# Offset parts of the norms behind the rotary tables, one row's norm offset on VectorE, and a nine-instruction inverse root in a two-layer decoder trunk

## The chip, the cores and the metric

The kernel runs on one core of a Trainium2 chip. Its engines are named as in the profile: PE (TensorE: matmuls and transposes), DVE (VectorE), ACT (ScalarE), POOL (GpSimd) and SP (SyncE, which here only issues transfers). Each engine takes its instructions in the order in which they were written into its queue. The metric is the time of one execution on the device in microseconds (us), the median of several runs.

## The reference

A trunk of two layers over 1024 tokens of width 1024, in float32. Layer 0 is a sparse attention: an indexer scores all earlier keys, each query keeps the best 256, and softmax attention runs on those. Layer 1 is a gated linear recurrence (HGRN2). Both are followed by a SwiGLU feed-forward part, and every part ends in a LayerNorm of `alpha * x + part(x)`. What the change touches:

```python
def layer_norm(x, g, b):
    mu = jnp.mean(xf, axis=-1, keepdims=True)
    var = jnp.mean(jnp.square(xf - mu), axis=-1, keepdims=True)
    return (xf - mu) * lax.rsqrt(var + LN_EPS) * g + b
...
def apply_rope(x, cos, sin):          # on the first dimensions of queries, keys and index keys
    return jnp.concatenate([x1 * cos - x2 * sin, x2 * cos + x1 * sin, x[..., 2 * half:]], axis=-1)
...
cos_q, sin_q = rope_tables(positions, ATT_ROT_DIM)      # from the positions, an input
c_q = rms_norm(c_q, g_cq)                               # another inverse root
k_idx = layer_norm(k_idx, g_ik, b_ik)
```

## The kernel before

The tokens lie in 8 row blocks of 128 (the partitions). Every float32 product is made of three products of rounded parts (lines 110 to 112, `mm3`), and the dense parts use a scheme of seven block products per 2 by 2 blocks, for which rows and weights are first added and subtracted in 512-column pieces and each result is split into a rounded part and a rest (lines 471 and 472, `split2`).

The program is written as Python generators that call engine instructions. A scheduling layer places the instructions of the engines' queues from the order of writing, with priorities and dependences; it also inserts the waits. So a shift in one place can shift neighbours on other engines.

**The start (`att_in`).** `rope_tables` (line 170) makes the cosine and sine tables: DVE reduces the angles, ACT takes the sine (line 206; the cosine first, then the sine), and POOL copies each table into its second half (line 207) and, twice, every other column into a shorter table (line 209). The shorter tables rotate the keys. Then a written list, `ORDER_IN`, sets the steps: `p` projects a row block (tile A), `f` transposes the next input rows, `k` handles the keys of a pair of row blocks. The key step takes an inverse root (`rsqrt`, line 114, tiles aih, aiy, ait), rotates the keys (`rope`, lines 221 to 225, tile rk), splits them (tile kk: ACT at line 1328, DVE at 1329) and lets PE transpose them (line 1343), then the normalized query part and the index keys (tile hc, lines 1351 and 1354). Ahead of each step of `ORDER_IN` one step of the generator `kits` is advanced.

**The offset parts (`kits`, line 378).** For two of the norms the bias b is later added to products by small matmuls instead of row by row. For that, POOL prepares five small tables in memory: first `select`, rows of ones (line 388, three transfers at 390), then four kits, two of them times a factor (line 399): load 4 rows (396), a difference and a negation (400, 401), and three times round to bfloat16 (404), store (405) and subtract (408). All use one work tile, `za`, so a step waits for the transfer of an earlier one. The tables are read by the feed-forward and later parts.

**The end of attention (`layer_norm`, line 135).** Rows 0 to 5 are normalized while the last attention blocks run, rows 6 and 7 after them. For each: DVE subtracts the mean and multiplies by g (line 151), ACT multiplies by the inverse root (152), POOL adds b in two halves (154). Then `enter` begins the first feed-forward part: `row_sums` (374, 375, tile gb) takes the sums of the row pairs (4, 6) and (5, 7) on DVE, and PE transposes rows and sums (line 352), whose split parts (tiles x_1617 to x_1620, one for each group of operands) feed the products.

**The inverse root (`rsqrt`).** It works on a few numbers per partition: scale and add eps (line 118), a first estimate from the bits of the number (119), three Newton steps of three instructions (121 to 123). Each depends on the one before. It is used at the four key pairs, the three groups of `layer_norm`, the norms of the later parts (`norm_scale`) and eight times in the recurrence (tile rm).

Of the kernel before, what the change touches and what calls it, by code (L numbers as in the profile page):

```python
# [18 lines left out]
ALU = mybir.AluOpType  # L19
# [48 lines left out]
class Core:  # L68
# [45 lines left out]
    def rsqrt(self, x, n, scale, eps, tag, eng=None):  # L114

        v = eng or self.nc.vector
        h, y, t = (self.tile(self.small, [P, max(n, 4)], F32, tag + x)[:, :n] for x in "hyt")
        v.tensor_scalar(h, x, scale, eps, op0=ALU.mult, op1=ALU.add)
        v.tensor_scalar(y.bitcast(I32), h.bitcast(I32), -0.5, 1597463007.0, op0=ALU.mult, op1=ALU.add)
        for _ in range(3):  # L120
            v.tensor_tensor(t, y, y, op=ALU.mult)
            v.scalar_tensor_tensor(t, t, -0.5, h, op0=ALU.mult, op1=ALU.mult)
            self.root = v.scalar_tensor_tensor(y, t, 1.5, y, op0=ALU.add, op1=ALU.mult)
        return y

    def pin(self, ins):
# [8 lines left out]
    def layer_norm(self, ts, g, b):  # L135

        nc, v = self.nc, self.nc.vector
        n = len(ts)
        mv = self.tile(self.small, [P, 4, 2], F32, "lnmv")[:, :n]
        for i, t in enumerate(ts):  # L140
            r = self.resid[:, t, :]
            st = self.tile(self.small, [P, 2, 6], F32, "lnst")
            for c in range(2):
                v.bn_stats(st[:, c, :], r[:, c * 512 : (c + 1) * 512])
            v.bn_aggr(mv[:, i, :], st.rearrange("p a b -> p (a b)"))
            yield
        rs = self.rsqrt(mv[:, :, 1], n, 1.0, LN_EPS, "ln")
        yield
        for i, t in enumerate(ts):
            r = self.resid[:, t, :]  # L150
            v.scalar_tensor_tensor(r, r, mv[:, i, 0:1], g, op0=ALU.subtract, op1=ALU.mult)
            nc.scalar.activation(r, r, AF.Copy, scale=rs[:, i : i + 1])
            for c in (slice(0, 512), slice(512, D)):
                nc.gpsimd.tensor_tensor(r[:, c], r[:, c], b[:, c], op=ALU.add)
            yield

    def row(self):
# [10 lines left out]
    def rope_tables(self, cp, wp, pt, it):  # L168

        nc, v = self.nc, self.nc.vector  # L170
        n = NT * 16
        pf = self.tile(wp, [P, NT], F32, "posf")
        v.tensor_copy(pf, pt)
        three = self.tile(wp, [P, 3, n], F32, "kk")
        ang, a1, a2 = (three[:, i, :] for i in range(3))
        v.tensor_tensor(
            ang.rearrange("p (t j) -> p t j", t=NT),
            pf.rearrange("p (t o) -> p t o", o=1).to_broadcast([P, NT, 16]),
            it.rearrange("p (o j) -> p o j", o=1).to_broadcast([P, NT, 16]),
            op=ALU.mult,  # L180
        )
        v.tensor_copy(a1.bitcast(F32R), ang)
        v.tensor_tensor(a2, ang, a1, op=ALU.subtract)
        turns = self.tile(wp, [P, 7, n], F32, "q")
        near = self.tile(wp, [P, 7, n], F32, "qi")
        for i, (a, p) in enumerate(((a1, 3), (a2, 2), (a1, 2), (a2, 1), (a1, 1), (a2, 0), (a1, 0))):
            v.tensor_scalar(turns[:, i, :], a, TURN[p], None, op0=ALU.mult)

        def frac(x, tmp, magic):
            v.tensor_scalar(tmp, x, magic, magic, op0=ALU.add, op1=ALU.subtract)  # L190
            v.tensor_tensor(x, x, tmp, op=ALU.subtract)

        frac(turns, near, 1.5 * 2.0**35)
        frac(turns, near, 1.5 * 2.0**23)
        u = turns[:, 0, :]
        for i in range(1, 7):
            v.tensor_tensor(u, u, turns[:, i, :], op=ALU.add)
        tabs = []
        for i, off in enumerate((0.25, 0.0)):
            w = turns[:, 1 + i, :]  # L200
            v.tensor_scalar(w, u, off, None, op0=ALU.add)
            frac(w, near[:, 0, :], 1.5 * 2.0**23)
            v.tensor_scalar(w, w, -0.4999999, 0.4999999, op0=ALU.max, op1=ALU.min)
            o, e = (self.tile(cp, [P, NT, 2, n], F32, f"rope{i}{n}") for n in (16, 8))
            w = w.rearrange("p (t j) -> p t j", t=NT)
            nc.scalar.activation(o[:, :, 0, :], w, AF.Sin, scale=2.0 * math.pi)
            nc.gpsimd.tensor_copy(o[:, :, 1, :], o[:, :, 0, :])
            for j in range(2):
                nc.gpsimd.tensor_copy(e[:, :, j, :], o[:, :, 0, 0:16:2])
            tabs.append((o, e))  # L210
        return zip(*tabs)

# [165 lines left out]
    def kits(self, pool, work, bs):  # L378

        nc, gp = self.nc, self.nc.gpsimd
        self.select = self.tile(self.kd, [12, 512], BF16, "select")
        self.kit = {}
        y = work[0:4, 0:256].bitcast(BF16)
        ones = self.ident[0:4, 0:4].rearrange("p (k o) -> p k o", o=1).to_broadcast([4, 4, P])
        gp.tensor_copy(y.rearrange("p (k c) -> p k c", k=4), ones)
        for j in range(3):
            gp.dma_start(self.select[4 * j : 4 * j + 4], y)  # L390
        yield
        rest, part = work[0:4, 0:512], work[0:4, 512:1024].bitcast(BF16)
        four = rest.rearrange("k (i c) -> k i c", i=4)
        for b, name, scale in bs:
            o = self.kit[name] = self.tile(self.kd, [12, 512], BF16, self.name(name[0]))
            gp.dma_start(four[:, 0:2, :], b.rearrange("(i k c) -> k i c", i=2, k=4))
            yield
            if scale is not None:
                gp.tensor_scalar(four[:, 0:2, :], four[:, 0:2, :], scale, None, op0=ALU.mult)
            gp.tensor_tensor(four[:, 2, :], four[:, 0, :], four[:, 1, :], op=ALU.subtract)  # L400
            gp.tensor_scalar(four[:, 3, :], four[:, 1, :], -1.0, None, op0=ALU.mult)
            for j in range(3):
                x = part[:, j % 2 * 512 : (j % 2 + 1) * 512]
                gp.tensor_copy(x, rest)
                gp.dma_start(o[4 * j : 4 * j + 4], x)
                yield
                if j < 2:
                    gp.tensor_tensor(rest, rest, x, op=ALU.subtract)
# [809 lines left out]
    def att_in(self, ap, csp, tp, x):  # L1218
        nc, v, gp, s = self.nc, self.nc.vector, self.nc.gpsimd, self.att
# [199 lines left out]

        does = dict(p=project, f=feature, k=keys, q=query, s=store, w=lambda _: query_weights(), a=lambda _: advance())  # L1420
        kits = self.kits(ap, self.tile(s.sel, [P, T], F32, "za"), s.bs)
        for step in self.ORDER_IN.split():
            next(kits, None)
            does[step[0]](int(step[1:] or 0))

    @staticmethod
# [608 lines left out]
```

## Time and profile before

| what | value |
|---|---|
| time, median of 3 runs | 2513.41 us (2510.82 to 2516.71) |
| the profiled execution | 2517.95 us, its span 2516.2 us |
| PE busy in the span | 2441.9 us |
| DVE busy | 1906.9 us |
| ACT busy | 1056.2 us |
| POOL busy | 176.9 us |

Times in profile rows count from the start of the span. A row of the order of time has the start, the duration, the engine, the line of the kernel, the instruction, its output and inputs with partitions x elements, how many follow each other (x), and in brackets how long the engine stood idle before it and which instruction ended that. Line numbers in rows of before are those of the kernel before; after the change, lines from `pin` on are 4 higher, up to `ORDER_IN`'s loop, and 5 higher behind it.

### The profile page before, as it was taken

How to read it: one execution, taken by the hardware profiler on the slowest of the kernel's cores; microseconds unless marked ns; L12 is line 12 of the kernel's file. 1: busy time of each engine (PE TensorE's matmuls, PEld its weight loads, DVE VectorE, ACT ScalarE, POOL GpSimd, SP SyncE). 2: the span in 40 equal slices, each digit the busy share in tenths (PEclk: the TensorE clock that was granted, in tenths of full speed). 3: DMA queues.
4: the chain of work that ended last, by engine and by line, in shares of the span. 5: the costliest groups of instructions: out<-in, count | busy, mean ns of one | idle time of the engine just before them, and what ended most of it. 6: DMA issues, size and time to landing. Idle time of an engine off the chain costs nothing.

```text
span 2516.2 us, 35546 instructions
## 1 busy us (share of the span) xinstructions
PE 2441.9 (97%) x12810; PEld 2041.3 (81%) x12810; DVE 1906.9 (76%) x3692; ACT 1056.2 (42%) x1972; POOL 176.9 (7%) x295
## 2 busy tenths in 40 slices
PE   6998999999999999999999999999999999999998
PEld 6887888888888888888788888887778888888886
DVE  6578776788997766566898888887889867665767
ACT  4467666564333333334443333333353333333431
POOL 6001002000000000000011111111000000000000
PEclk8998999999999999999999999999999999999999
DMA  3337001011895332665431111113638733326853
GB/s 133 109 125 240 26 22 56 18 47 71 291 328 176 94 120 92 236 217 195 144 104 47 55 43 55 43 55 110 230 122 293 267 101 93 121 92 235 281 183 117
DMA packets 140127, 338.94 MB, mean 135 GB/s; under 512 B 17288, under 2 KB 18088, under 8 KB 132264
## 3 DMA queue, kind: packets, MB, share of 16 engines
q1 hardware_dynamic: 137224, 329.19, 38.6%
q0 software_dynamic: 2720, 7.42, 1.0%
q8 instruction: 101, 1.65, 0.3%
q14 instruction: 82, 0.67, 0.1%
HBM read 232.15 MB, written 104.39 MB: 134 GB/s over the span
## 4 chain that ended last, share of the span: by engine, by line
PE 64%; issue 10%; DVE 5%; DMA 2%; ACT 1%; POOL 1%; SPq 0%; DVEq 0%; ACTq 0%; POOLq 0%
PE Y L112 11%; PE Y L110 11%; PE Y L111 11%; PE M L111 8%; PE M L112 8%; PE M L110 7%; PE M L1082 3%; PE M L352 1%; DVE w L472 1%; DMA raw<-in_wd_dram 1%; PE M L1067 1%; PE M L1144 1%; PE M L1131 1%; PE M L1146 1%; PE M L354 0%
## 5 line engine op out<-in xcount | busy, mean ns | idle before, releaser
L471 ACT CAST w<-raw 128x512 fp32r<-128x512 f32 (+1 forms) x373 | 288.3, 775 | 527.7 <-PE Y L112 273.8
L472 DVE TENSOR_TENSOR w<-raw,w 128x512 fp32r<-128x512 f32 (+1 forms) x373 | 327.1, 881 | 180.8 <-ACT w L471 178.6
L110 PE MATMUL Y<-x,w 128*128 128x512 f32 (+1 forms) x1120 | 433.2, 387 | 1.8 <-DVE rows L789 0.7
L111 PE MATMUL Y<-x,w 128*128 128x512 f32 (+1 forms) x1120 | 429.9, 384 | 0.0
L112 PE MATMUL Y<-x,w 128*128 128x512 f32 (+1 forms) x1120 | 428.1, 382 | 0.0
L111 PE MATMUL M<-x,w 128*128 128x512 f32 (+1 forms) x644 | 245.7, 382 | 3.3 <-DVE x L472 3.3
L110 PE MATMUL M<-x,w 128*128 128x512 f32 (+1 forms) x644 | 245.6, 381 | 0.1
L110 PEld LDWEIGHTS Y<-x,w 128*128 128x128 f32 x1120 | 211.8, 189 | 41.3 <-ACT w L471 1.2
L112 PE MATMUL M<-x,w 128*128 128x512 f32 (+1 forms) x644 | 245.2, 381 | 0.0
L112 PEld LDWEIGHTS Y<-x,w 128*128 128x128 f32 x1120 | 211.8, 189 | 39.2 <-issue 0.9
L111 PEld LDWEIGHTS Y<-x,w 128*128 128x128 f32 x1120 | 211.9, 189 | 37.1 <-issue 0.2
L471 ACT CAST w<-s 128x512 fp32r<-128x512 f32 x180 | 111.8, 621 | 303.6 <-PE Y L112 116.5
L472 DVE TENSOR_TENSOR w<-s,w 128x512 fp32r<-128x512 f32 x180 | 124.4, 691 | 52.0 <-ACT w L471 51.1
L111 PEld LDWEIGHTS M<-x,w 128*128 128x128 f32 x644 | 121.6, 189 | 26.6 <-DVE x L472 3.7
L110 PEld LDWEIGHTS M<-x,w 128*128 128x128 f32 x644 | 121.5, 189 | 24.3 <-ACT x L471 1.2
L112 PEld LDWEIGHTS M<-x,w 128*128 128x128 f32 x644 | 121.6, 189 | 22.8
L110 PE MATMUL Y<-w 128*128 128x512 f32 x284 | 111.8, 394 | 0.2 <-ACT ph L471 0.2
L111 PE MATMUL Y<-w,w 128*128 128x512 f32 x284 | 111.4, 392 | 0.1
L112 PE MATMUL Y<-w,w 128*128 128x512 f32 x284 | 111.4, 392 | 0.0
L111 PE MATMUL M<-w,w 128*128 128x512 f32 x248 | 97.0, 391 | 1.3 <-DVE w L472 1.3
L112 PE MATMUL M<-w,w 128*128 128x512 f32 x248 | 96.9, 391 | 0.0
L110 PE MATMUL M<-w 128*128 128x512 f32 x248 | 96.1, 391 | 0.2 <-ACT ph L471 0.2
(497 smaller groups left out, 5112.4 us busy)
## 6 DMA issues: line engine op xcount, KB each, us to landing
raw<-in_wgu_dram SPq DMA_DIRECT2D x44, 1024.0 KB, 6.1
wdt<-in_wd_dram SPq DMA_DIRECT2D x44, 512.0 KB, 5.2
raw<-in_wd_dram SPq DMA_DIRECT2D x66, 256.0 KB, 4.2
raw<-in_hw_dram SPq DMA_DIRECT2D x16, 1024.0 KB, 4.8
qd<-qx SPq DMA_DIRECT2D x16, 512.0 KB, 3.6
qt<-qd SPq DMA_DIRECT2D x64, 128.0 KB, 2.7
t5q<-wdt SPq DMA_DIRECT2D x26, 256.0 KB, 3.7
t7q<-wdt SPq DMA_DIRECT2D x26, 256.0 KB, 2.7
```

What stands on the lines that cost most here:

```text
L110: mm(out, a[0], b[0], start=first, stop=False, **kw)
L111: mm(out, a[0], b[1], start=False, stop=False, **kw)
L112: mm(out, a[1], b[0], start=False, stop=last, **kw)
L352: mm(y[:, c], x[:, c], self.ident, **flags)
L471: self.nc.scalar.copy(hi, x)
L472: ins = (eng or self.nc.vector).tensor_tensor(lo, x, hi.bitcast(F32), op=ALU.subtract)
L1067: nc.tensor.matmul(pl[:, n, :], kk[:, m : m + P], y[:, n, :], start=True, stop=True)
L1082: nc.tensor.matmul(pl[rows, n, cols], lhs, rhs, start=True, stop=True)
L1131: nc.tensor.matmul(pd[:, n, :], kt[:, n, :], vt[:, n, :], start=True, stop=True)
L1144: nc.tensor.matmul(po[:, n, :], at[:, n, :], vt[:, n, :], start=True, stop=states[n] is None)
L1146: nc.tensor.matmul(po[:, n, :], qd[:, n * P : (n + 1) * P], states[n], start=False, stop=True)
```

## The change

Three edits. First, the first instruction of `kits` is ordered behind the last rotary copy on POOL, and the first six steps of `ORDER_IN` no longer advance `kits`. Second, row 7's bias in `layer_norm` is added by DVE instead of POOL. Third, `rsqrt` has nine instructions instead of eleven: the number is scaled by 64/9, one Newton step is taken, and then one step of third order, whose constant absorbs the scale.

```diff
         h, y, t = (self.tile(self.small, [P, max(n, 4)], F32, tag + x)[:, :n] for x in "hyt")
-        v.tensor_scalar(h, x, scale, eps, op0=ALU.mult, op1=ALU.add)
+        k = 64.0 / 9.0
+        v.tensor_scalar(h, x, scale * k, eps * k, op0=ALU.mult, op1=ALU.add)
         v.tensor_scalar(y.bitcast(I32), h.bitcast(I32), -0.5, 1597463007.0, op0=ALU.mult, op1=ALU.add)
-        for _ in range(3):
-            v.tensor_tensor(t, y, y, op=ALU.mult)
-            v.scalar_tensor_tensor(t, t, -0.5, h, op0=ALU.mult, op1=ALU.mult)
-            self.root = v.scalar_tensor_tensor(y, t, 1.5, y, op0=ALU.add, op1=ALU.mult)
+        v.tensor_tensor(t, y, y, op=ALU.mult)
+        v.scalar_tensor_tensor(t, t, -0.5, h, op0=ALU.mult, op1=ALU.mult)
+        v.scalar_tensor_tensor(y, t, 1.5, y, op0=ALU.add, op1=ALU.mult)
+        v.tensor_tensor(t, y, y, op=ALU.mult)
+        v.tensor_tensor(h, t, h, op=ALU.mult)
+        v.scalar_tensor_tensor(t, h, -10.0 / 3.0, h, op0=ALU.add, op1=ALU.mult)
+        self.root = v.scalar_tensor_tensor(y, t, 5.0, y, op0=ALU.add, op1=ALU.mult)
         return y
...
             for c in (slice(0, 512), slice(512, D)):
-                nc.gpsimd.tensor_tensor(r[:, c], r[:, c], b[:, c], op=ALU.add)
+                (v if t == 7 else nc.gpsimd).tensor_tensor(r[:, c], r[:, c], b[:, c], op=ALU.add)
             yield
...
             for j in range(2):
-                nc.gpsimd.tensor_copy(e[:, :, j, :], o[:, :, 0, 0:16:2])
+                self.roped = nc.gpsimd.tensor_copy(e[:, :, j, :], o[:, :, 0, 0:16:2])
...
-        gp.tensor_copy(y.rearrange("p (k c) -> p k c", k=4), ones)
+        self.behind(gp.tensor_copy(y.rearrange("p (k c) -> p k c", k=4), ones), self.roped)
...
-        for step in self.ORDER_IN.split():
-            next(kits, None)
+        for i, step in enumerate(self.ORDER_IN.split()):
+            if i > 5:
+                next(kits, None)
             does[step[0]](int(step[1:] or 0))
```

What this does to the queues, at three places.

POOL, at the start. Before, the rotary copies (L207 and L209) stand within the third kit (stored to `o_131`):

```order
L405 DMA o_131_682<-za_292 4x512
L207 COPY rope_76_276<-rope_76_276 128x8x16
L209 COPY rope_77_277<-rope_76_276 128x8x8 x2
L408 TENSOR_TENSOR za_292<-za_292 4x512
L404 CAST za_292<-za_292 4x512
L405 DMA o_131_682<-za_292 4x512
L408 TENSOR_TENSOR za_292<-za_292 4x512
L404 CAST za_292<-za_292 4x512
L207 COPY rope_78_286<-rope_78_286 128x8x16
L209 COPY rope_79_287<-rope_78_286 128x8x8 x2
```

After, they stand right behind the few instructions that prepare masks, and the rows of ones and all kits follow:

```order
L1668 AFFINE_SELECT bias_13_85<-bias_13_85 128x128
L211 COPY rope_76_276<-rope_76_276 128x8x16
L213 COPY rope_77_277<-rope_76_276 128x8x8 x2
L211 COPY rope_78_286<-rope_78_286 128x8x16
L213 COPY rope_79_287<-rope_78_286 128x8x8 x2
L392 CAST za_292<-ident 4x512
L394 DMA select_525<-za_292 4x512 x3
L400 DMA za_292<-in_lnb_dram 4x2x128
L404 TENSOR_TENSOR za_292<-za_292 4x128
```

The copies moved ahead of `select` and of two and a half kits. The loads of the index queries (tile `it`) stand behind the last kit in both orders.

DVE, at the first keys. Before, five instructions of the first inverse root stand ahead of the rotation (L221, which reads the short sine table `rope_79`) and the root's last three between the rotation's:

```order
L122 SCALAR_TENSOR_TENSOR ait_477<-ait_477,aih_475 128x4
L123 SCALAR_TENSOR_TENSOR aiy_476<-ait_477,aiy_476 128x4
L121 TENSOR_TENSOR ait_477<-aiy_476 128x4
L122 SCALAR_TENSOR_TENSOR ait_477<-ait_477,aih_475 128x4
L123 SCALAR_TENSOR_TENSOR aiy_476<-ait_477,aiy_476 128x4
L221 TENSOR_TENSOR rk_466<-hc_348,rope_79_287 128x64
L121 TENSOR_TENSOR ait_477<-aiy_476 128x4
L1320 BN_STATS kist_709<-hc_601 128x6
L222 TENSOR_TENSOR hc_348<-hc_348,rope_77_277 128x2x2x16
L122 SCALAR_TENSOR_TENSOR ait_477<-ait_477,aih_475 128x4
L224 TENSOR_TENSOR hc_348<-hc_348,rk_466 128x2x2x8
```

After:

```order
L122 SCALAR_TENSOR_TENSOR ait_460<-ait_460,aih_458 128x4
L123 SCALAR_TENSOR_TENSOR aiy_459<-ait_460,aiy_459 128x4
L124 TENSOR_TENSOR ait_460<-aiy_459 128x4
L125 TENSOR_TENSOR aih_458<-ait_460,aih_458 128x4
L126 SCALAR_TENSOR_TENSOR ait_460<-aih_458 128x4
L225 TENSOR_TENSOR rk_449<-hc_343,rope_79_287 128x64
L127 SCALAR_TENSOR_TENSOR aiy_459<-ait_460,aiy_459 128x4
L1324 BN_STATS kist_688<-hc_580 128x6
L226 TENSOR_TENSOR hc_343<-hc_343,rope_77_277 128x2x2x16
L1336 SCALAR_TENSOR_TENSOR hc_343<-hc_343,aiy_459,gcq_189 128x256
L228 TENSOR_TENSOR hc_343<-hc_343,rk_449 128x2x2x8
```

One instruction of the root is left behind the rotation's first, and a scaling of the query part (L1336) came ahead of its end.

DVE, at the end of attention (gb are the row sums, x_1617 to x_1620 the split operands). Before:

```order
L472 TENSOR_TENSOR x_1617_10378<-Y_10541,x_1617_10378 128x4x128
L509 TENSOR_TENSOR raw_10412<-raw_10412,M_10516 128x256
L374 TENSOR_TENSOR gb_10624<-resid_2201 128x512
L375 TENSOR_TENSOR gb_10624<-gb_10624,resid_2201 128x512
L472 TENSOR_TENSOR x_1619_10380<-Y_10562,x_1619_10380 128x4x128
L374 TENSOR_TENSOR gb_10627<-resid_2201 128x512
L472 TENSOR_TENSOR x_1619_10380<-Y_10569,x_1619_10380 128x4x128
L472 TENSOR_TENSOR x_1620_10381<-Y_10589,x_1620_10381 128x4x128
L375 TENSOR_TENSOR gb_10627<-gb_10627,resid_2201 128x512
```

After, with the two adds of row 7 at L158:

```order
L378 TENSOR_TENSOR gb_10610<-resid_2193 128x512
L158 TENSOR_TENSOR resid_2193<-resid_2193,gb_2228 128x512 x2
L513 TENSOR_TENSOR raw_10398<-raw_10398,M_10502 128x256
L476 TENSOR_TENSOR x_1617_10364<-Y_10527,x_1617_10364 128x4x128
L476 TENSOR_TENSOR x_1619_10366<-Y_10548,x_1619_10366 128x4x128
L476 TENSOR_TENSOR x_1619_10366<-Y_10555,x_1619_10366 128x4x128
L476 TENSOR_TENSOR x_1620_10367<-Y_10575,x_1620_10367 128x4x128
L379 TENSOR_TENSOR gb_10610<-gb_10610,resid_2193 128x512
L378 TENSOR_TENSOR gb_10613<-resid_2193 128x512
```

The second operand of x_1617 moved from ahead of the first row sum to behind it and the adds, and the other row sums moved behind the operands. PE reads x_1617 ahead of x_1619 in both orders.

## The prediction

> **What bounds the kernel now.** I read the page's first lines, then the list of waits on PE over the whole program, then the order of time around the longest of them on each engine.
>
> ```profile
> span 2516.2 us, 35546 instructions
> PE 2441.9 (97%) x12810; PEld 2041.3 (81%) x12810; DVE 1906.9 (76%) x3692; ACT 1056.2 (42%) x1972; POOL 176.9 (7%) x295
> ```
>
> PE is busy for 97% of the span, so an edit on DVE or POOL pays only where PE stands still. The list of who waited for whom (total us, times, longest us), PE's rows:
>
> ```profile
> PE C L1343 <- ACT kk L1328: 15.9, 1, 15.9
> PE M L352 <- ACT rows L907: 5.4, 2, 3.0
> ...
> PE M L111 <- DVE x L472: 3.3, 1, 3.3
> ```
>
> One wait of 15.9 us, about a fifth of all the time PE is idle, is by far the longest. The order of time around it (start us, us, engine, line, instruction, in brackets the idle time before it and what ended it), one engine after the other:
>
> ```profile
> 36.07 0.33 PE L111 MATMUL A<-winl,xsh 128*128 128x384 f32 x1
> 52.33 1.97 PE L1343 MATMUL C<-ident,kk 128*128 128x128 f32 x8 [15.93 <-ACT kk L1328]
> ...
> 39.81 0.16 DVE L123 SCALAR_TENSOR_TENSOR aiy<-ait,aiy 128x4 f32<-128x4 f32 x1
> 50.52 0.23 DVE L221 TENSOR_TENSOR rk<-hc,rope 128x64 f32<-128x64 f32 x1 [10.55 <-POOL rope L209]
> ...
> 38.82 0.31 ACT L206 ACTIVATE rope<-q 128x128 f32<-128x128 f32 x1 [3.95 <-DVE q L203]
> ...
> 49.29 0.60 POOL L404 CAST za<-za 4x512 bf16<-4x512 f32 x1
> 49.84 0.28 POOL L207 COPY rope<-rope 128x128 f32<-128x128 f32 x1
> 50.08 0.41 POOL L209 COPY rope<-rope 128x64 f32<-128x64 f32 x2
> ```
>
> The sine table is finished on ACT at 39.13, but POOL copies it only at 49.84 to 50.49, since the instructions of the offset parts (tile za) stand ahead of it on the in-order queue. DVE, with nothing left to do from 39.97, waits 10.55 us for that copy, and the key transposes on PE wait behind DVE and ACT.
>
> **The change part by part.** All terms are gains in us, made against the profiled execution (2517.95 us, its span 2516.2 and 1.75 around it); that stands 4.54 above the median of 2513.41, and I take the sum off the median, since no term is a share of the total.
>
> A, rotary copies ahead of the offset parts. POOL now copies as soon as the sine is there: 0.65 us for its three copies (49.84 to 50.49). With nothing else changed that is 39.8, DVE starts the rotation at 40.0 instead of 50.5, and PE the transposes at 52.33 - 10.5 + 0.4 = 42.2 (the new order puts one scaling of 128x256, 0.4 us, ahead of the rotation's end); the stall from 36.4 is then 5.8. But DVE gets faster too, since POOL is empty up to then:
>
> ```profile
> 21.08 1.48 DVE L190 TENSOR_SCALAR qi<-q 128x896 f32<-128x896 f32 x1
> 24.50 0.61 DVE L190 TENSOR_SCALAR qi<-q 128x896 f32<-128x896 f32 x1
> 33.35 0.21 DVE L203 TENSOR_SCALAR q<-q 128x128 f32<-128x128 f32 x1
> 33.62 1.12 DVE L119 TENSOR_SCALAR aiy<-aih 128x4 int32<-128x4 int32 x1
> 37.62 1.17 DVE L203 TENSOR_SCALAR q<-q 128x128 f32<-128x128 f32 x1
> 89.94 0.16 DVE L119 TENSOR_SCALAR aiy<-aih 128x4 int32<-128x4 int32 x1
> ...
> 37.18 1.52 POOL L408 TENSOR_TENSOR za<-za 4x512 f32<-4x512 f32 x1
> ```
>
> The same instruction takes 1.48 and 0.61, 1.17 and 0.21, 1.12 and 0.16; the long ones stand beside POOL's (the 1.17 one ends at 38.79, POOL's at 38.70). Without them DVE saves 0.87 + 0.96 + 0.96 = 2.8, all of it ahead of the sine. The sine then ends at 36.3, the copies at 37.0, the rotation starts at 37.0 and the transposes at 39.2: a stall of 2.8 in place of 15.9, so A = 13.1. Bounds: 10.1 (DVE no faster) and 15.9 (no stall at all). What is late next is DVE's own chain, which reaches the rotation at about that time.
>
> B, the clock behind the stall. The stretches show PE's granted clock in the column after the engines' busy times (then DMA share, GB/s):
>
> ```profile
> 52.30:57.00 4.70, 4.67 (x19) 4.58 (x20) 3.11 (x10) 1.64 (x5) 3.48 (x5) 0.50 0.00 1
> 579.00:583.00 4.00, 3.79 (x10) 2.97 (x11) 3.73 (x7) 1.39 (x3) 0.00 (x0) 0.57 0.01 4
> ...
> 579.22 0.65 PE L110 MATMUL L<-xh,oth 128*128 128x512 f32 x1 [0.68 <-ACT oth L229]
> ```
>
> After the long stall PE ran 4.7 us at half clock, a loss of 2.35. A stall of 2.8 lies between that and the one of 0.68 at 579.2, behind which the clock was 0.57 as well. I take half, B = 1.2, with 0 and 2.35 as ends. The Trainium skill (TensorE: Matmul & The Clock Gate, "What's actually happening") says the clock halves after an idle window of about 3.4 us; by it a stall of 2.8 could leave the clock full, B would be 2.35 and the sum 1.15 larger. This trace goes against it at 579, where far shorter idle time was followed by a low clock, so I don't rely on it.
>
> C, the offset parts now run beside the keys. They must stand somewhere: four kits, about 50 us of POOL, move from 4 to 62 us to the time behind the copies.
>
> ```profile
> 57.37 1.00 DVE L221 TENSOR_TENSOR rk<-hc,rope 128x64 f32<-128x64 f32 x1
> 59.99 1.03 DVE L224 TENSOR_TENSOR hc<-hc,rk 128x32 f32<-128x32 f32 x1
> 71.12 0.23 DVE L221 TENSOR_TENSOR rk<-hc,rope 128x64 f32<-128x64 f32 x1
> 65.00:100.00 35.00, 34.57 (x212) 31.44 (x212) 23.68 (x85) 14.05 (x33) 0.83 (x2) 1.00 0.12 46
> ```
>
> The rows at 57.37 and 71.12 are the same step of the rotation with and without an offset part beside it: 0.77 lost, and the smaller step at 59.99 loses as much or more. With a third of their kind that makes about 2 us in the 11.5 of the last kit, an estimate, so 6 in the 35 us that newly overlap. In the 65 to 100 stretch, which will carry most of it, PE is full but DVE is idle for 11.3 of 35, so most of the loss is absorbed; I take a third as reaching PE. C = -2.0, ends 0 and -6.
>
> D, the loads queued behind the kits. POOL's queue also issues the loads of the index queries (tile it), and they now stand behind all kits by less room.
>
> ```profile
> 3.77 1.79 POOL L390 DMA_DIRECT2D select<-za  x3
> 40.21 0.65 POOL L396 DMA_DIRECT2D za<-in_lnb_dram  x1
> 50.97 0.65 POOL L396 DMA_DIRECT2D za<-in_lnb_dram  x1
> 61.95 0.54 POOL L405 DMA_DIRECT2D p<-za  x1 [0.29 <-POOL za L404]
> 99.17 1.12 POOL L1441 DMA_DIRECT2D it<-id  x2 [36.68 <-DMA id<-qx]
> ...
> 109.32 0.42 PE L110 MATMUL C<-kih,it 128*128 128x384 f32 x1
> ```
>
> A kit without a factor took 10.8 (40.21 to 50.97, of which 1.2 were the rotary copies), one with it 11.5 (50.97 to 62.49). Four of them are 2 x 9.6 + 2 x 11.5 = 42.2, the rows of ones ahead of them 6 as an estimate (three issues of 0.6 at 3.77 and their landing), so the kits end near 37.0 + 48 = 85. The store that the loads wait for is over at 99.17 - 13 = 86, and the first product on them had no wait at 109.32, some 5 us after they can have landed (about 4 after the issue). Cost D = 0; with a kit pace as long as before (58.7 in all) they end at 96, 5 us past the slack of 91, the other end: -5. The six steps of the key stage that no longer advance a kit emit nothing else, so they cost nothing.
>
> E, row 7's offset on DVE. The end of the attention stage:
>
> ```profile
> 600.00 5.88 POOL L154 TENSOR_TENSOR resid<-resid,gb 128x512 f32<-128x512 f32 x4 [74.52 <-ACT resid L152]
> 601.34 1.75 DVE L374 TENSOR_TENSOR gb<-resid 128x512 f32<-128x512 f32 x1 [0.87 <-POOL resid L154]
> 605.92 0.69 DVE L374 TENSOR_TENSOR gb<-resid 128x512 f32<-128x512 f32 x1 [0.56 <-POOL resid L154]
> 606.53 1.28 DVE L472 TENSOR_TENSOR x<-Y,x 128x512 fp32r<-128x512 f32 x2
> 607.27 0.58 PE L111 MATMUL M<-x,w 128*128 128x256 f32 x1 [3.33 <-DVE x L472]
> ```
>
> POOL's four halves take 5.88, DVE waits twice for them and then owes PE the operand that ends at 607.2. Now DVE does two adds of 0.69 (the plain price of a 128x512 sum, at 605.92) behind its first sum, and only two of the halves stay on POOL. From 600.9 (the root is 0.4 earlier): sum 0.7, adds 1.4, a 128x256 subtraction 0.4, three operands of 0.6 = 605.2, or 606.3 when the first sum stays at 1.75. PE's wait doesn't vanish: the second half of operand x_1617 now stands behind the adds, so PE waits for it at some 604, in its new order, instead of for x_1619 at 607.2. Gain 0.9 to 2.0; E = 1.5. The low end is -1 (both adds lengthened by POOL beside them), the high one 3.3, the whole wait.
>
> F, the roots. Of 24 roots, two instructions fall off each; each step of such a chain is
>
> ```profile
> 2509.78 0.16 DVE L121 TENSOR_TENSOR lnt<-lny 128x1 f32<-128x1 f32 x1
> 2509.98 0.16 DVE L122 SCALAR_TENSOR_TENSOR lnt<-lnt,lnh 128x1 f32<-128x1 f32 x1
> ```
>
> 0.20 apart, so 0.39 a root. On the path are the last root of the program (nothing runs but DVE and the store behind it) and the two behind which PE waits for the normalized rows (5.4 us in two waits in the list above): F = 3 x 0.39 = 1.2. The first root of the keys is inside A. The others hide behind PE's products; if that cover were gone they would add at most 20 x 0.39 = 7.8, but PE's list shows no wait there of that size. The mixer's eight roots feed POOL, whose waits cost PE nothing in it. A few heads around 400 us stand in a slightly other order on all engines: 0, give or take 1.
>
> Sum: 13.1 + 1.2 - 2.0 + 0 + 1.5 + 1.2 = 15.0. 2513.4 - 15.0 = **2498.4 us** (2503 for an execution like the profiled one).
>
> **The rivals.** First, DVE is no faster beside an idle POOL, because its long instructions had other reasons: A = 10.1, time 2501.4. Against it stand four row pairs with POOL's ends beside them.
>
> Second, the clock stays full behind the shorter stall, B = 2.35: 2497.3. For it speaks the stall's size, against it the stretch at 579. The Trainium skill's page on the clock gate, cited above, would give this one.
>
> Third, slower: the kits take POOL's queue so long that the index loads are late. The place is PE's first product on tile it; it decides nothing until the kits end at 91, then each us costs one, so the whole gain is gone at 106, that is when the kits take 69 us instead of the 58.7 of before; at 112 the time is 2519. For it: DVE is busier in the new place (23.7 of 35 us) and the two lengthen each other (POOL's 1.52 above). Against it: the transfers the kits wait for fall into a stretch with 46 GB/s, the last column of the 65 to 100 row. A milder form, ends at 94, gives 2501.4. The Trainium skill (SBUF — State Buffer, "Who interferes with whom") says that a transfer issued by GpSimd waits for its descriptors while VectorE holds the port they share; the kits' issues at 61.95 and before show 0.5 to 0.7 beside a working DVE, so the trace bears little of it out.
>
> Fourth, the change doesn't do what it says: the copies are early, but the sine itself or a weight split sets the rotation, and at least 10 of the 15.9 us stay. Then A is at most 5.9 and B 0: 2513.4 - 6.6 = 2506.8 or later. Against it stands 38.82, the sine's own start.
>
> **How the numbers follow.** Forecast 0.52; DVE no faster 0.13; clock full 0.14; kits late but below the gain 0.08, and past it 0.04; copies not the last wait 0.09. What tells a change from none here is 0.2%, 5.0 us, or 2508.4. Faster: all but the slower case and most of the fourth, 0.89; within 0.2%: 0.07; slower 0.04. The low end is all upper bounds (15.9 + 2.35 + 0 + 0 + 3.3 + 1.2 = 22.8): 2490.6. The high end takes in the second and third cases and the near half of the fourth: 2507.
>
> **What would show it.** Right: the wait of PE L1347 (the transposes' new line) under 6 us and DVE's wait for the rotary copies under 1; POOL's copies near 36 us, its kits until 82 to 91; the index product of tile it without a wait above 2; PE's wait at 604 on x of 1 to 3 us; the span 13 to 17 shorter, nearly all of it before 100 us. Wrong: a new wait of PE on tile it, C's stall in the second pair of keys above 6 us, or a rotation that starts later than 40.

## The result and the profile after

| kernel | runs | median us | range us | ratio to before (95% interval) |
|---|---|---|---|---|
| before | 7 | 2513.26 | 2510.82 to 2518.57 | 1 |
| after | 7 | 2498.90 | 2498.13 to 2505.43 | 0.9948 (0.9934 to 0.9962) |

The change makes the kernel 14.4 us faster by the medians (9.5 to 16.6 by the interval of the ratio). The profiled execution of after took 2498.84 us (span 2497.0), 19.1 less than that of before, so the two profiles overstate the difference by some 5 us; how far two profiles of one program differ is said below.

The waits of PE over the whole program, after (total us, times, longest us):

```profile
PE B L1400 <- DVE qx L234: 4.0, 1, 4.0
...
PE M L111 <- DVE x L476: 2.4, 1, 2.4
...
PE C L1347 <- DVE xsl L234: 1.4, 1, 1.4
...
PE C L1347 <- ACT kk L1332: 1.0, 1, 1.0
```

The wait of 15.9 us at the first key transposes is down to 1.0 (last row). Two waits for DVE are new or have grown: 4.0 us at the transposes of the query (L1400), where before had 0.35, and 1.4 us at those of the second pair of keys, where before had none. The wait on row 7's operand went from 3.3 to 2.4. The rows of before at the query (L1396 there), the second of which has lost its wait in after:

```profile
96.30 0.66 PE L1396 MATMUL B<-ident,q 128*128 128x128 f32 x4 [0.35 <-DVE qx L230]
106.80 0.66 PE L1396 MATMUL B<-ident,xin 128*128 128x128 f32 x4 [1.23 <-DVE qx L230]
```

The order of time at the start of after, on ACT, POOL, DVE, PE and POOL again:

```profile
33.83 0.31 ACT L210 ACTIVATE rope<-q 128x128 f32<-128x128 f32 x1 [0.24 <-DVE q L207]
...
34.49 0.42 POOL L213 COPY rope<-rope 128x64 f32<-128x64 f32 x2
34.86 0.60 POOL L392 CAST za<-ident 4x512 bf16<-4x512 f32 x1
...
34.95 0.60 DVE L225 TENSOR_TENSOR rk<-hc,rope 128x64 f32<-128x64 f32 x1 [0.19 <-POOL rope L213]
...
37.40 1.18 PE L1347 MATMUL C<-ident,kk 128*128 128x128 f32 x8 [1.04 <-ACT kk L1332]
...
82.01 0.54 POOL L409 DMA_DIRECT2D p<-za  x1 [0.29 <-POOL za L408]
86.30 1.13 POOL L1446 DMA_DIRECT2D it<-id  x2 [3.75 <-DMA id<-qx]
```

The second sine starts at 33.83 instead of 38.82, the copies are over at 34.9, the rotation starts at 34.95 instead of 50.52, and the transposes at 37.40 instead of 52.33. The kits run from 34.86 to 82.6, and the index loads behind them still wait 3.75 us for their own data, so the queue does not delay them.

Matching the same matmuls of both profiles, after stands ahead of before by 17.0 us at before's 58, by 18.7 at 64, 16.8 at 80 to 95, 11.6 at 103, 13.1 at 110, 14.5 at 125, 15.0 at 200 and 17.2 at 625. Most of the gain is made and partly given back within the first 110 us. The 1.4 between 110 and 125 come at a place that the change does not touch: PE's clock was low there in before and full in after, behind waits for the index loads that are much the same in both (0.78 and 1.80 us in before, 0.66 and 2.09 in after). PE's stretches behind these waits, before and after (the granted clock, that is the share of full speed that PE was given, is the column ahead of the last two):

```profile
118.00:122.00 4.00, 3.98 (x14) 4.00 (x15) 1.24 (x2) 0.98 (x2) 0.83 (x2) 0.58 0.31 83
...
105.00:109.00 4.00, 3.94 (x22) 3.97 (x23) 1.24 (x2) 0.98 (x2) 0.83 (x2) 1.00 0.31 85
```

### The profile page after: what moved, and what is told of

Read it like the earlier page. It is cut to its first block, busy times and chain, and to the rows that moved or that the text cites. A ratio compares the mean times of both kernels' runs of the same rounds, so it can differ in the third digit from the quotient of the medians.

```text
span 2497.0 us, 35500 instructions
## 1 busy us (share of the span) xinstructions
PE 2437.4 (98%) x12810; PEld 2037.8 (82%) x12810; DVE 1902.7 (76%) x3646; ACT 1056.0 (42%) x1972; POOL 170.6 (7%) x293
## 4 chain that ended last, share of the span: by engine, by line
PE 75%; DVE 7%; issue 4%; DMA 3%; ACT 2%; SPq 0%; POOL 0%; DVEq 0%; ACTq 0%; POOLq 0%
PE Y L112 10%; PE Y L111 10%; PE Y L110 10%; PE M L111 8%; PE M L110 8%; PE M L112 8%; PE O L1850 3%; PE M L1086 2%; PE L L1879 2%; PE O L1793 1%; PE M L356 1%; PE T L1845 1%; DVE w L476 1%; DMA wdt<-in_wd_dram 1%; PE W L112 1%
```

## The experiments

All ratios are to the kernel before, run on the same chip in the same session; its medians were 2515.51, 2516.12 and 2516.42 us in the three sessions.

| kernel | median us | ratio (95% interval) |
|---|---|---|
| e1_kits: kits behind the copies, alone | 2502.74 | 0.9951 (0.9938 to 0.9964) |
| e2_row7: row 7's offset on DVE, alone | 2512.69 | 0.9990 (0.9981 to 0.9999) |
| e3_roots: nine-instruction root, alone | 2513.94 | 0.9993 (0.9984 to 1.0003) |
| e4_copies_dve: copies on DVE, kits at the start | 2506.14 | 0.9961 (0.9947 to 0.9976) |
| e7_kits_stretch: after, kits longer by transfers | 2510.39 | 0.9978 (0.9965 to 0.9991) |
| e8_kits_120: after, kits behind the eighth index load | 2500.45 | 0.9935 (0.9919 to 0.9950) |
| e9_late_dve: the same, copies on DVE | 2500.70 | 0.9947 (0.9933 to 0.9962) |
| e11_kits_16: after, kits over 16 partitions | 2497.41 | 0.9925 (0.9911 to 0.9939) |
| e12_after_again: after | 2503.32 | 0.9948 (0.9935 to 0.9960) |

### One part at a time

e1_kits is before with these edits alone:

```diff
-                nc.gpsimd.tensor_copy(e[:, :, j, :], o[:, :, 0, 0:16:2])
+                self.roped = nc.gpsimd.tensor_copy(e[:, :, j, :], o[:, :, 0, 0:16:2])
-        gp.tensor_copy(y.rearrange("p (k c) -> p k c", k=4), ones)
+        self.behind(gp.tensor_copy(y.rearrange("p (k c) -> p k c", k=4), ones), self.roped)
-            next(kits, None)
+            if i > 5:
+                next(kits, None)
```

> The kernel before with one part of the change alone: the rope tables' copies stand ahead of the kits on GpSimd, the kits start behind them. Theory 1 (this part carries the change): the first key transposes wait under 2 us instead of 15.9, two new waits for VectorE of 1 to 4 us (second keys near 48, query transposes near 83) give 4 to 5 back, and the time is 12 to 14 us under the kernel before, near 2500. Theory 2 (the parts of the change lean on each other, the row and the roots carry a third or more of it): 8 us or less, 2505 or more. Without the new root VectorE has two more small instructions ahead of each split, so the two new waits may be 0.3 us longer than with it.

Theory 1 holds: a ratio of 0.9951 is 12.3 us. PE's waits there, with the query's new one first:

```profile
PE B L1396 <- DVE qx L230: 3.5, 1, 3.5
...
PE C L1343 <- ACT kk L1328: 1.4, 1, 1.4
```

The gain and most of the giving back belong to this one part. Of the two new waits that theory 1 named, the one at the second keys is smaller than it said (0.8 us), and one of 1.6 at the index keys (0.6 in before) stands beside it.

e2_row7 is before with the choice `(v if t == 7 else nc.gpsimd)` alone, e3_roots before with the new root alone.

> The kernel before with one part of the change alone: the offset of row 7's norm is added on VectorE instead of GpSimd. Theory 1 (the prediction's E): TensorE's wait of 3.3 us on the row at 607 shrinks by 0.5 to 1.5 us and the later stages keep that: 0.5 to 1.5 us under the kernel before, near 2512. Theory 2 (only moved): the wait goes from one row to the next thing that is late and the time is the same within 0.3 us.

> The kernel before with one part of the change alone: each inverse root in nine instructions in place of eleven. Theory 1 (the prediction's F): three roots stand on the path, 0.39 us each, so the time is 1.2 us under the kernel before, near 2512. Theory 2: none of the roots' two instructions is on the path for long, and the time is the same within 0.4 us.

Row 7 alone gives 2.5 us (0.3 to 4.8 by the interval). The middle lies above what theory 1 said, and the interval takes its range in. The first product on x after the wait in e2_row7, then PE's stretch behind it in before and in e2_row7 (PE, PEld, DVE, ACT, POOL busy, then PE's granted clock):

```profile
602.82 0.39 PE L111 MATMUL M<-x,w 128*128 128x256 f32 x1 [1.61 <-DVE x L472]
...
607.20:611.50 4.30, 4.23 (x23) 4.01 (x24) 2.28 (x6) 1.07 (x2) 0.00 (x0) 0.66 0.19 77
602.80:607.00 4.20, 3.92 (x29) 3.45 (x30) 4.20 (x8) 2.15 (x4) 0.00 (x0) 1.00 0.22 89
```

The wait shrank by 1.7 us (3.33 to 1.61), and behind the shorter wait the clock stayed full, where it was 0.66 before. In the profiles e2_row7's lead over before grows from 2.7 us at 577 to 5.2 at 625, so by 2.5 at the place itself. The 2.7 ahead of it do not come from the edit; a part is the clock at 118 to 122, which is 1.00 in e2_row7 and 0.58 in before. The prediction priced the wait and not the clock behind it.

The roots alone give 1.8 us by the ratio, with an interval from 4.0 faster to 0.8 slower: in line with F's 1.2, not separated from nothing. Its profile shows something that neither theory had. The wait at the first key transposes was 12.9 us instead of 15.9:

```profile
PE C L1347 <- ACT kk L1332: 12.9, 1, 12.9
```

There the kits ahead of the copies had run 2.8 us earlier on POOL (one of their casts took 0.62 us in place of 1.55). If that came in every execution the times should be 3 us lower or more, which they are not clearly; it stays open.

### The place in the queue, or DVE's speed

e4_copies_dve leaves the kits at the start and takes the copies out of POOL's queue in another way:

```diff
-            nc.gpsimd.tensor_copy(o[:, :, 1, :], o[:, :, 0, :])
+            v.tensor_copy(o[:, :, 1, :], o[:, :, 0, :])
-                nc.gpsimd.tensor_copy(e[:, :, j, :], o[:, :, 0, 0:16:2])
+                v.tensor_copy(e[:, :, j, :], o[:, :, 0, 0:16:2])
```

> The kernel before with the rope tables' six copies moved from GpSimd to VectorE; the kits stay at the start, beside VectorE's first rows, and neither the row nor the roots are changed. It tells apart two causes of the gain at the first key transposes. Cause 1 (the place in GpSimd's queue): the copies no longer stand behind the kits, VectorE has them as soon as the sines are there, but its rows are still lengthened by GpSimd, so the rotation starts near 42 to 45 instead of 50.5, the transposes wait 7 to 9 us, and TensorE is at a low clock for some us behind them; no new wait near 48 or 83, since the kits are past by then. The time is 7 to 10 us under the kernel before, 2503 to 2506. Cause 2 (VectorE's speed beside GpSimd): nearly all of the gain is that VectorE runs alone, so with the kits in place the rotation starts at 46 or later and the time is less than 6 us under the kernel before.

Cause 1 holds: 9.8 us faster by the ratio, the top of its range. The copies, the rotation and PE's wait, then the clock behind it:

```profile
36.83 1.17 DVE L207 COPY rope<-rope 128x128 f32<-128x128 f32 x1
37.92 0.71 DVE L209 COPY rope<-rope 128x64 f32<-128x64 f32 x2
...
41.17 0.21 DVE L221 TENSOR_TENSOR rk<-hc,rope 128x64 f32<-128x64 f32 x1
...
43.16 1.11 PE L1343 MATMUL C<-ident,kk 128*128 128x128 f32 x4 [6.20 <-ACT kk L1328]
...
43.10:47.00 3.90, 3.84 (x17) 3.67 (x17) 3.90 (x9) 1.06 (x5) 3.25 (x5) 0.50 0.01 1
```

With the kits still beside it DVE reaches the rotation at 41.17, of which these copies take 1.8 and those of the second table 0.4. In e1_kits, with POOL idle, the same old root and the copies on POOL, it reached it at 35.85. So the place is worth 9.8 us here, net of the copies' time on DVE, and DVE's free run about another 3 to 5 at the rotation, more than the 2.8 that the prediction had. The remaining stall of 6.2 us cost the clock as well.

### The new waits: GpSimd beside VectorE, or the new order

The two new waits follow rows on DVE that are longer than their kind. After at both places, DVE, the row of POOL beside it, and PE:

```profile
46.96 1.00 DVE L119 TENSOR_SCALAR aih<-sq 128x4 f32<-128x4 f32 x1
46.78 1.15 POOL L412 TENSOR_TENSOR za<-za 4x512 f32<-4x512 f32 x1
48.61 0.66 PE L1347 MATMUL C<-ident,kk 128*128 128x128 f32 x4 [1.41 <-DVE xsl L234]
...
76.84 1.38 DVE L1336 SCALAR_TENSOR_TENSOR hc<-hc,aiy,gcq 128x256 f32<-128x256 f32 x1
80.00 1.26 DVE L1341 TENSOR_TENSOR hc<-hc,bik 128x256 f32<-128x256 f32 x1
79.53 1.44 POOL L412 TENSOR_TENSOR za<-za 4x512 f32<-4x512 f32 x1
83.27 0.92 PE L1400 MATMUL B<-ident,q 128*128 128x128 f32 x4 [3.96 <-DVE qx L234]
```

The row at 46.96 handles 4 elements per partition and ends at 47.96; POOL's row beside it ends at 47.93. The one at 80.00 ends at 81.26 beside POOL's end at 80.97. In both pairs DVE's row ends just behind POOL's, whatever its size, so it seems to wait for it. The Trainium skill (SBUF — State Buffer, "Who interferes with whom") says that whichever of the two holds the pair of ports they share keeps it for its whole instruction; the rows agree.

e12_after_again is after once more:

> The changed kernel once more, unchanged, timed on the same chip as the kernel with the kits over 16 partitions, for its second profile. Theory 1 (the two new waits belong to the program): VectorE's late rows make TensorE wait again near 48 and near 83, 4 to 6 us in all, and the wait at the first key transposes is again near 1 us; the ratio to the kernel before is again 0.994 to 0.9955. Theory 2 (they belong to one execution): the waits are at other places or differ by more than 2 us in all.

Theory 1: both waits came again, with the same sizes (4.0 and 1.4 us, one each), and the ratio is the same.

e8_kits_120 moves the kits away:

```diff
-        self.behind(gp.tensor_copy(y.rearrange("p (k c) -> p k c", k=4), ones), self.roped)
+        self.behind(gp.tensor_copy(y.rearrange("p (k c) -> p k c", k=4), ones), self.fetched)
-            if i > 5:
+            if i > 30:
-            s.fetch.dma_start(it.bitcast(F32), s.ids[j][:, k])
+            self.fetched = s.fetch.dma_start(it.bitcast(F32), s.ids[j][:, k])
```

> The changed kernel with the kits taken out of the stretch 35 to 83 us: they start behind the eighth index load, near 117 us, and run to about 165, where TensorE has products with data that is already held. Theory 1 (the two new waits for VectorE come from GpSimd's work beside it): TensorE's waits of 1.4 us near 48.6 and 4.0 us near 83.3 go down to under 0.5 and 0.5 to 1.5 us, VectorE's rows there have their short durations (0.16 for the small root operations, 0.76 for the two products of the keys), 3 to 5 us are gained and all kept: near 2495. Theory 2 (the waits come from the new order on VectorE, the rotation's rows ahead of the split): the waits stay within 1 us and the time is the same within 1 us. Theory 3 (the kits at 117 to 165 cost there what they cost at 35 to 83): the waits go, and new ones of the same size come between 117 and 175; the time is the same within 1 us.

Theory 2 falls: with the same rows in the same order on DVE at the query, those rows are short and the query's wait is 0.7 us in two parts. The wait at the second keys is gone as well.

```profile
76.61 0.48 DVE L1336 SCALAR_TENSOR_TENSOR hc<-hc,aiy,gcq 128x256 f32<-128x256 f32 x1
78.45 0.43 DVE L1341 TENSOR_TENSOR hc<-hc,bik 128x256 f32<-128x256 f32 x1
...
PE B L1400 <- DVE qx L234: 0.7, 2, 0.4
```

For the time the profile speaks for theory 3. Against after the matmuls gain 3.5 us between 60 and 95, and lose 4.2 between 120 and 180, where the kits now lie and where after, from 121 on, has no wait at PE above 0.2. Four waits of e8_kits_120 there add up to 2.1 us of the loss, and the rest is not traced to rows; the two longest:

```profile
130.88 0.41 PE L1358 MATMUL C<-ident,hc 128*128 128x128 f32 x2 [0.56 <-DVE ks L1350]
155.09 0.44 PE L110 MATMUL C<-kih,xsh 128*128 128x384 f32 x1 [1.03 <-ACT rel L1461]
```

The times do not decide: the ratio of 0.9935 is 3.3 us under after's 0.9948, as theory 1 would have it, but the intervals overlap, and e9_late_dve, with the kits at the same late place, has 0.9947. That moving the work did not remove its price is therefore a reading of one profile of each.

e9_late_dve adds the copies on DVE.

> As the kernel with the kits behind the eighth index load, and the six rope copies on VectorE besides, which now has GpSimd idle beside it. Four copies of 0.21 and 0.29 us (durations of the run with the copies on VectorE and the kits at the start) stand in VectorE's queue in place of a hand-over to GpSimd and 1.6 us of copies there. Theory 1: the hand-over goes, the rotation starts 0.3 to 1.0 us earlier than at 34.95 and TensorE's wait at the first key transposes falls from 1.04 us toward 0.3: 0.3 to 0.8 us under the kernel with late kits. Theory 2: the first sines, at 33.3, set the rotation either way, and the copies lengthen VectorE's chain by as much as the hand-over took: the same within 0.3 us.

Theory 1 has no support: the rotation starts at 36.82 against 36.68 in e8_kits_120, and not ahead of 34.95, and the ratios cannot be told apart.

e11_kits_16 leaves the kits at their place and makes their instructions shorter:

```diff
-        rest, part = work[0:4, 0:512], work[0:4, 512:1024].bitcast(BF16)
+        rest, part = work[0:16, 0:128], work[0:16, 512:640].bitcast(BF16)
-            gp.dma_start(four[:, 0:2, :], b.rearrange("(i k c) -> k i c", i=2, k=4))
+            gp.dma_start(four[:, 0:2, :], b.rearrange("(i k a c) -> (k a) i c", i=2, k=4, a=4))
-                gp.dma_start(o[4 * j : 4 * j + 4], x)
+                gp.dma_start(o[4 * j : 4 * j + 4].rearrange("k (a n) -> (k a) n", a=4), x)
-        self.nc.sync.dma_start(o.rearrange("p i c -> p (i c)"), self.kit[name])
+        k = self.kit[name].rearrange("p (a i c) -> p a i c", a=4, i=4)
+        for a in range(4):
+            self.nc.sync.dma_start(o[:, :, a * 32 : (a + 1) * 32], k[:, a])
```

> The changed kernel with the kits laid over 16 partitions in place of 4, at the same place in GpSimd's queue, their arithmetic on 128 elements of each partition instead of 512; their three parts are stored in that layout and fetched later by four transfers each instead of one. Rows of the changed kernel: a 4x512 subtraction takes 1.15 us, a 4x128 one 0.45; a 4x512 cast 0.60. So GpSimd's arithmetic in the kits falls from some 23 us to some 10, their waits on transfers stay, and they end near 70 instead of 82.6. Theory 1 (the new waits are the time of GpSimd's arithmetic beside VectorE, wherever it lies: 3.5 us gained with the kits gone from there, and 4.2 us lost where they were put): the waits of 1.4 us near 48.6 and 4.0 near 83.3 fall by half or more, and 2 to 3 us are gained against the changed kernel on the same chip and kept, if the additional small transfers later on are hidden. Theory 2 (the number of GpSimd's instructions beside VectorE counts, not their length): the waits stay within 1 us and the time is the same within 1 us.

Theory 1 holds for the waits, as the kits' POOL rows, the index loads and PE's waits show:

```profile
43.68 0.42 POOL L412 TENSOR_TENSOR za<-za 16x128 f32<-16x128 f32 x1
...
70.58 0.52 POOL L409 DMA_DIRECT2D p<-za  x1 [0.29 <-POOL za L408]
81.51 1.10 POOL L1448 DMA_DIRECT2D it<-id  x2 [10.41 <-DMA id<-qx]
...
PE C L1349 <- ACT kk L1334: 1.0, 1, 1.0
...
PE B L1402 <- DVE qx L234: 0.4, 1, 0.4
```

The subtraction fell from 1.15 to 0.42 us, the cast from 0.60 to 0.28; the wait at the query fell from 4.0 to 0.4, the one at the second keys (1.4) is gone, and at 110 us the matmuls stand 5.3 ahead of after's. The median is 5.9 us under that of after in the same session, but that is not clear of the spread: the intervals around 0.9925 and 0.9948 overlap, as does that of e8_kits_120. The profiles show the lead at the start (5.7 at 200 us) and not at the end, since the two profiled executions took 2498.83 and 2498.84 us. How much of the lead is kept, and what the added small transfers cost later, stays open.

### The queue's price, and the kernel before again

e7_kits_stretch issues each of the kits' four loads three times:

```diff
-            gp.dma_start(four[:, 0:2, :], b.rearrange("(i k c) -> k i c", i=2, k=4))
+            for _ in range(3):
+                gp.dma_start(four[:, 0:2, :], b.rearrange("(i k c) -> k i c", i=2, k=4))
```

> The changed kernel with the kits made longer and nothing added to their arithmetic: each of the kits' four loads of a bias row is issued three times, each waiting for the one before (2.1 us of issue and landing each by the changed kernel's rows at 49.44 to 51.78), so the kits end near 99.5 instead of 82.6. Theory 1 (the prediction's D, its price from a point on): the index loads, which were due 3.75 us after the kits' last store, are issued near 100 instead of 86.3; the first index product, at 96.2 with no wait, then waits 8 to 11 us for them, the other index loads follow, and the time is 7 to 11 us over the changed kernel, near 2508. Theory 2 (the loads have far more room than the 3.75 us, since TensorE has other work to take there): no wait for them over 2 us and the time within 2 us of the changed kernel. If the longer stretch moves the waits of 1.4 us near 48.6 and 4.0 us near 83.3, GpSimd's arithmetic beside VectorE is what made them.

Theory 1, with the wait in two pieces, since the scheduler put two of the index loads ahead of the last kit's arithmetic:

```profile
105.22 0.54 POOL L410 DMA_DIRECT2D p<-za  x1 [0.29 <-POOL za L409]
105.75 1.13 POOL L1447 DMA_DIRECT2D it<-id  x2
...
98.40 0.42 PE L110 MATMUL C<-kih,it 128*128 128x384 f32 x1 [2.67 <-DMA it<-id]
109.24 0.66 PE L110 MATMUL C<-kih,it 128*128 128x384 f32 x1 [6.36 <-DMA it<-id]
```

The first index loads were issued at 93.67, the next pair at 105.75. The kits ended at 105.8, later than the 99.5 expected. The ratio went from 0.9948 to 0.9978, some 7.5 us. The waits at the keys and the query moved: none at the second keys (1.4 in after), 1.8 us in two at the query, and a new 2.1 in two at the transposes behind the keys.

e10_before_again is the kernel before, for a second profile (2517.56 us):

> The kernel before once more, unchanged, for one more profile of it: it shows how much of the 19.1 us between the two profiled executions (the medians differ by 14.4) is the execution itself. Theory 1: a part of the start is not the same in every execution, the wait at the first key transposes is 12 to 16 us (12.9 in the kernel with the new roots alone), and the matmuls behind 1750 us stand 2 to 4 us earlier than in the first profile. Theory 2: the start repeats within 0.5 us and only the late part, behind 1250 us, moves.

Theory 2: the start repeats.

```profile
PE C L1343 <- ACT kk L1328: 16.0, 1, 16.0
```

Up to 580 us every matmul stands within 0.2 us of its place in the first profile. Behind that the two profiles drift apart by +1.4 at 600, -3.9 at 1100 and +0.4 at the end, in the same program. The first step, at 579, is the clock: with the same two waits of 0.8 and 0.7 us ahead of it, PE got 0.57 in the first profile and 1.00 in the second.

```profile
579.00:583.00 4.00, 3.79 (x16) 2.94 (x17) 3.85 (x8) 1.38 (x3) 0.00 (x0) 1.00 0.01 4
```

So shifts behind 580 us of a few us between two single profiles say nothing about the change, and the gain is read from the medians instead of the 19.1 us.

## Why the prediction was right, step by step

The forecast was 2498.4 us and the time 2498.9. The mechanism was right: the copies behind the offset parts held up the first keys, and moving them ahead took nearly the whole stall away. That the sum came out to half a microsecond is luck, since A and B were too small, C too small as a cost, E too large, and a gain came that no term has.

- **A, right in mechanism, undersized.** The wait went from 15.93 to 1.04, a gain of 14.9 where 13.1 stood. What was mis-sized is DVE's speed-up ahead of the rotation: the prediction took 2.8 from its pairs of long and short rows (it shows three; the rivals speak of four), and the second sine came 5.0 earlier (33.83 instead of 38.82). How much of it is the shorter root is not shown: the rotation starts at 35.85 in e1_kits with the old root, and at 34.95 to 36.82 in after, e8_kits_120 and e9_late_dve with the new one. e4_copies_dve shows that DVE's delay by POOL was real, and that the place in the queue was the larger part.
- **B, undersized, and not for the second rival's reason.** Behind the stall of 1.04 the clock was full (1.00 in the stretch from 37.40 to 41.00), so all of the 2.35 came back. The rival asked for a full clock behind a stall of 2.8, which did not occur; here B was right in size because A was larger. The Trainium skill (TensorE: Matmul & The Clock Gate, "What's actually happening") has the clock drop after an idle window of about 3.4 us: the stall of 1.04 agrees, but stalls of 1.98 and 2.42 us, shorter than that as well, left the clock at 0.68 and 0.61. The prediction's own evidence, 0.57 at 579, was that of one execution: e10_before_again has 1.00 there. A and B together are 17.2, which the matmuls' 17.0 at 58 us confirms; 14.3 had been forecast.
- **C, undersized by about half.** From 17.0 at 58 to 13.1 at 110 the loss is 3.9 net where 2.0 stood. On the way it was larger: from 18.7 (before has two small waits for DVE beside its last kit, 1.1 us in all, that after has not) down to 11.6, which is past the bound of 6; the 1.5 up to 110 come back where before waits 1.23 us at 106.80. The step that failed is "I take a third as reaching PE": it averaged DVE's idle time over 35 us, but the loss reached PE at two splits that DVE owed it at once. The price includes a low clock behind the wait of 3.96 (0.64 in the stretch from 83.30 to 88.00).
- **D, right.** The kits ended at 82.6 (85 was forecast), and the first product on the loads (96.22) had no wait. The longest wait for an index load in after, 2.09 at 105.06, is just past the sign's 2, but it is not new: before waits 1.80 at the same product. e7_kits_stretch shows that the cliff is there: 23 us later costs 7.5 us, less than one for one, since part of the loads slipped ahead.
- **E, in its range, oversized.** PE's wait on x is 2.42 in after, in the stated 1 to 3, so the wait gave 0.9 where 1.5 stood. Alone the part gave 2.5 us: 1.7 by the wait, and its 1.61 was followed by a full clock; in after the clock behind 2.42 was 0.61.
- **F, consistent, not shown.** The 1.2 lies within e3_roots' interval, which also holds zero.
- **A gain that no term has.** The 1.4 us between 110 and 125, from a clock that was low in before, in both of its profiles (0.58 and 0.57), and full in both profiles of after. It need not come from the change, since e2_row7, which is the kernel before up to 580 us, has 1.00 there too.

The three parts alone sum to 16.6 us against 13.1 by after's own ratio, each uncertain by 2 to 4 us, so the times can't show whether the parts lean on each other. The wait on row 7's operand shows that two of them do: it is 1.61 us with the row alone, 2.6 with the roots alone and 2.4 with all three, so on top of the roots the row took only 0.2 off it. Why is open.

## What to carry to other kernels

When work moves to another stretch on GpSimd, its cost is not its idle slot but the VectorE rows it stops there; price it at the row where TensorE waits for VectorE next, not at VectorE's mean load. If no stretch is free, shorten the single GpSimd instruction (more partitions, fewer elements each) rather than move it again: here the second move gained nothing that the times can tell, while the shorter instructions took the 4.0 us wait down to 0.4 (their 5.9 us by the medians is not clear of the spread). A wait that shrinks can also save the low clock behind it, as in e2_row7; count that as a chance, not as a sure gain.

## What was not expected of the hardware

The clock behind a stall does not follow from the stall's length alone. PE's stretches behind six stalls:

```profile
37.40:41.00 3.60, 3.60 (x24) 3.13 (x25) 3.50 (x13) 1.64 (x5) 0.81 (x2) 1.00 0.02 4
587.70:592.00 4.30, 4.24 (x23) 4.24 (x24) 3.00 (x6) 0.00 (x0) 0.00 (x0) 0.61 0.29 115
83.30:88.00 4.70, 4.70 (x21) 4.60 (x22) 1.80 (x6) 0.59 (x1) 1.13 (x2) 0.64 0.63 237
...
38.50:43.00 4.50, 4.24 (x21) 3.83 (x22) 3.87 (x14) 1.85 (x6) 0.00 (x0) 0.68 0.00 0
...
38.10:42.00 3.90, 3.53 (x24) 3.21 (x25) 3.57 (x12) 1.96 (x7) 0.00 (x0) 1.00 0.00 0
...
98.40:103.00 4.60, 4.47 (x21) 3.54 (x21) 3.11 (x6) 3.42 (x7) 3.88 (x6) 1.00 0.53 208
```

The first three are after: a stall of 1.04 left it at 1.00, 2.42 and 3.96 at 0.61 and 0.64. Then e8_kits_120, where 1.98 was followed by 0.68, e9_late_dve, where 1.58 at the same place was followed by 1.00, and e7_kits_stretch, where 2.67 was followed by 1.00 for 4.6 us. Shorter stalls are no safer: before has 0.50 from 214.2 to 217.6, behind a stall of 0.87 us at 212.93. And the two waits at 579 left 0.57 in one execution of before and 1.00 in the other. So no length divides the two cases here. The Trainium skill (TensorE: Matmul & The Clock Gate, "What's actually happening") says that the window in which activity is judged runs freely, which fits that 1.98 tips it and 2.67 does not; its idle window of some 3.4 us is longer than most stalls that tipped it here, so a window need not be idle throughout.

GpSimd is lengthened by VectorE too: in e8_kits_120 a pair of copies of 0.42 us took 1.64 beside a VectorE row of 1.22, which is part of why the rotation there began at 36.68 instead of 34.95.

```profile
34.23 1.64 POOL L213 COPY rope<-rope 128x64 f32<-128x64 f32 x2
34.23 1.22 DVE L1261 TENSOR_TENSOR w_iql<-sc,w_iqh 128x1024 fp32r<-128x1024 f32 x1
```
